# A planned one-core decoder trunk: first loads on two DMA queues in smaller weight pieces, the last row tile in two column halves

## The chip, the cores and the metric

The kernel runs on one core of one Trainium2 chip. The metric is the device time of one execution in microseconds (us); shorter is better. The other seven cores are idle.

## The reference

One layer of a hybrid decoder trunk works on 1,024 prompt tokens and 64 sample tokens (8 sequences of 8), each of width 1,024. Everything is float32.

```
h    = rms_norm(x, norm_g)
proj = h @ w_in                                   # 1024 x 3088: a, gl, zc, q, k, v, zg, lr
u    = a * sigmoid(gl)                            # causal depthwise convolution of width 31 over u,
cv   = silu(group_layer_norm(conv(u)))            # then group LayerNorm, silu and a 512 x 512 product
cv   = (cv @ w_pw + b_pw) * silu(zc)
o    = gated_linear_attention(q, k, v, gates(lr)) # 4 heads, chunked, exact recurrence
o    = rms_norm_per_head(o) * gla_g * silu(zg)
y    = rms_norm(x + concat[cv, o] @ w_out, final_g)
```

Outputs are y, the last 30 rows of u for the prompt and for each sample sequence, and the final attention states.

## The kernel before, in words

Tokens lie in three chunks of columns: `CHUNKS = [(0, 384), (384, 384), (768, 320)]`. The third, `FIRST = 2`, is worked on first. Every matrix is split in two float32r parts (h_ and l_ for weights, hh and hl for activations). ScalarE (ACT) copies the high part, VectorE (DVE) subtracts to get the low part, and TensorE (PE) makes three products for each block of 128 rows: hh by h, hl by h, hh by l.

**Order.** The instructions are not written in their final order. `prog.add` collects them with a priority (the place in the program), and `schedule` (L188) plans an order for each engine from cost estimates: `LAT`, `IN` and `SAME` are latencies in ns, SP is the queue of DMA issues, `STICK` lets TensorE go on with the same type of matmul rather than switch, and `DVE_PACE` lengthens VectorE's estimates. The order planned is what each engine then runs, strictly in turn. Operations that need an activation table are chained in program order (`self.chain`), so that a table is loaded no more often than the program's text demands.

**The start (L1004 to L1026).** Ten matmuls on zeros warm TensorE (tile `warm`). All loads go out on SP. For each half h of the depth and each of four weight tiles (gl and a of column tiles 0 and 1), the loop loads one block of x for `FIRST` (`x_load`, 160 KB), one weight half (`whalf`, four blocks of 128 rows, 256 KB, tile s_gl or s_a) and splits both (`raw_split`: hh on ACT and hl on DVE, from x times norm_g, without the norm; `load_split`: h_ on ACT, l_ on DVE). Four staging tiles `wst` hold weight halves; the last two halves go into `big` tiles. `rms_scale(c)` squares x on ACT (tile sq), adds squares on DVE, sums over partitions with float32 matmuls (tile ms), and makes rs[c] with Ln and Exp on ACT. The products of `FIRST` are scaled by rs afterwards: `gl_chunk` and `a_chunk` with early=True multiply by rs, take the sigmoid and multiply again. Chunks 0 and 1 are normalised first (`rms_split`: x times norm_g times rs on DVE, then a split) and need rs of their chunk. Loads of chunk 1 are held until a matmul of rs[FIRST] has run.

**The end (L1211 to L1350).** The output product is made from seven products of half matrices (pr1 to pr7), 48 matmuls of 512 columns each; the last is pr4, added by `product` into the PSUM banks acc[0..3] (tile ya), one bank for each of the row tiles 4 to 7. `y_first` handles one column half of a row tile: square with a row sum on ACT, multiply by fg (final_g) on DVE, a small operation on ss. `y_last` handles the other half: square with row sum, Ln and Exp for the row's scale, one `scalar_tensor_tensor` on DVE for its own half y, an ACT copy with the scale for the finished half z, and two stores to out_y, both on SP. The last loop goes over the row tiles 4, 5, 6, 7; the last half of tile 6 is stored after tile 7's sum is made (argument `after`).

Of the kernel before, what the change touches and what calls it, by code (L numbers as in the profile page):

```python
# [6 lines left out]
F32 = mybir.dt.float32  # L7
# [128 lines left out]
class Program:  # L136
# [51 lines left out]
    def schedule(self):  # L188
        import heapq
        from bisect import bisect_left, insort  # L190
        LAT = {"PE": 197 + MARGIN, "DVE": 130 + MARGIN, "ACT": 143 + MARGIN, "POOL": 150, "SP": 900}
        IN = {"PE": 129, "DVE": 0, "ACT": 0, "POOL": 0, "SP": 50}
        SAME = {"PE": 0, "DVE": 127, "ACT": 150, "POOL": 60, "SP": 900}
        free_at = {t: [0.0] * n for t, n in self.slots.items()}
        pend = {t: [] for t in self.slots}
        for o in self.ops:
# [14 lines left out]
        table = [next(o.table for o in self.ops if o.table is not None)]  # L211
        tile_end = {}
        holder = {}
        dma = [0.0, 0.0]
        done = []
        kind = [None]

# [12 lines left out]
            return True  # L230

        def cross(d, o):
            if d.eng == o.eng:
                return SAME[o.eng]

            return LAT[d.eng] + IN[o.eng] + (SLACK if o.eng == "PE" and d.eng != "SP" and d.end > SLACK_FROM else 0)

        while events:
            t, e = heapq.heappop(events)
            if t < t_free[e]:  # L240
                continue
            best = same = None
            nxt = None
            for o in avail[e]:
                if o.ready <= t:
                    if (best is None or o.prio < best.prio) and can_alloc(o, t):
                        best = o
                    if (e == "PE" and o.kind == kind[0] and (same is None or o.prio < same.prio)
                            and can_alloc(o, t, True)):
                        same = o  # L250
                elif nxt is None or o.ready < nxt:
                    nxt = o.ready
            if best is None:
                if nxt is not None:
                    heapq.heappush(events, (nxt, e))
                continue

            if same is not None and same.prio < best.prio + STICK:
                best = same
            o = best  # L260
            avail[e].remove(o)
            o.start = t
            cost = o.cost
            if o.table is not None and table[0] != o.table:
                table[0] = o.table
                cost += 1300
            if e == "PE" and o.kind != kind[0]:
                kind[0] = o.kind
                cost += 90
            if e == "SP":  # L270
                t_free[e] = t + 60
                dma[0] = max(dma[0], t) + 450
                dma[1] = max(dma[1], dma[0] + 650) + o.bytes / 360.0
                o.end = dma[1]
            else:
                if e == "DVE":
                    cost *= DVE_PACE
                o.end = t + cost + o.lag
                t_free[e] = t + cost
            done.append(o)  # L280
            for tl in o.tiles:
                if tl.tag in free_at and tl.slot is None:
                    o.allocs.append(tl)
                    k = min(range(len(free_at[tl.tag])), key=lambda i: free_at[tl.tag][i])
                    free_at[tl.tag][k] = float("inf")
                    tl.slot = k
                    tl.before = holder.get((tl.tag, k))
                    holder[(tl.tag, k)] = tl
                    del pend[tl.tag][bisect_left(pend[tl.tag], tl.first)]
                    for e2 in LAT:  # L290
                        heapq.heappush(events, (max(t, t_free[e2]), e2))
            for tl in o.tiles:
                tl.left -= 1
                tile_end[tl] = max(tile_end.get(tl, 0.0), o.end + LAT[e])
                if tl.left == 0 and tl.tag in free_at:
                    free_at[tl.tag][tl.slot] = tile_end[tl]
                    for e2 in LAT:
                        heapq.heappush(events, (max(tile_end[tl], t_free[e2]), e2))
            for u in o.users:
                u.ready = max(u.ready, o.end + cross(o, u))  # L300
                u.wait -= 1
                if u.wait == 0:
                    avail[u.eng].append(u)
                    heapq.heappush(events, (max(u.ready, t_free[u.eng]), u.eng))
            heapq.heappush(events, (t_free[e], e))
# [25 lines left out]
def build(tc, A, O):  # L331
# [9 lines left out]
    def R(v):  # L341
        return v.ap() if isinstance(v, View) else v
# [47 lines left out]
    def zero(out):  # L390
        fill(out, 0.0)

    def dma(out, in_, late=False):
        v = out if isinstance(out, View) else in_
        if late:
            prog.hold = late
        prog.add("SP", lambda: nc.sync.dma_start(R(out), R(in_)), [out], [in_], 0,  # L397
                 nbytes=v.n * 4 * (v.part[1] - v.part[0]))

    def dma_add(out, in_):  # L400
# [19 lines left out]
    with ctx:  # L420
# [37 lines left out]
        def pc(i, n=1):  # L458
            return par[:, i:i + n]
# [20 lines left out]
        hl = [[None] * 3 for _ in range(KT)]  # L480
        xs = {}

        def x_load(c, ks=range(KT), late=False):
            t0, n = CHUNKS[c]
            for k in ks:
                xk = rows("x", k, F32)[:, t0:t0 + n]
                dma(xk, A["xT"][:, k, t0:t0 + n], late)
                xs[(c, k)] = xk

        row_tiles = {}  # L490
# [36 lines left out]
            act(rs[c], ms, AF.Ln, bias=eps)  # L527
            act(rs[c], rs[c], AF.Exp, scale=-0.5)

        def rms_split(c):  # L530
            n = CHUNKS[c][1]
            for k in range(KT):
                xk = xs[(c, k)]
                stt(xk, xk, pc(C_NG + k), rs[c], ALU.mult, ALU.mult)
                hh[k][c], hl[k][c] = part("hh", k, c), part("hl", k, c)
                split(hh[k][c], hl[k][c], xk)
# [10 lines left out]

        def whalf(kind, i, h, stage=None):
            return load_split(f"{kind}{i}_{h}", A["w_in"][mt[(kind, i)]][:, 4 * h:4 * h + 4, :], 4, P, stage)

        def wtile(kind, i):
            return [whalf(kind, i, h) for h in range(2)]
# [448 lines left out]
                mix_samples(4 + i, o[:, 256:n])  # L1001


        dma(par, A["par"])  # L1004
        w0, w1 = [[], []], [[], []]
        for h in range(2):
            for i, (w, kind, ct) in enumerate(((w0[0], "gl", 0), (w0[1], "a", 0), (w1[0], "gl", 1), (w1[1], "a", 1))):
                x_load(FIRST, range(4 * h + i, 4 * h + i + 1))
                w.append(whalf(kind, ct, h, stage=big if 4 * h + i >= STAGE else None))
                raw_split(range(4 * h + i, 4 * h + i + 1))  # L1010
        rms_scale(FIRST)
        x_load(0)
        x_load(1, late=True)
        rms_scale(0)
        for ct, w in enumerate((w0, w1)):
            gl_chunk(ct, w[0], FIRST, True)
            a_chunk(ct, w[1], FIRST, True)
        rms_split(0)
        rms_scale(1)
        rms_split(1)  # L1020
        w_rank = gate_load()
        for c in (0, 1):
            for ct, w in enumerate((w0, w1)):
                gl_chunk(ct, w[0], c)
                a_chunk(ct, w[1], c)
        rms_split(FIRST)  # L1026
        for ct in range(CT):
            dma(u_s[ct][:, :, 0:CW - 1], A["cc"][:, ct], late=True)
        dma(cst, A["cst"], late=True)
# [169 lines left out]
                bv.append(parts(f"{name}b", i, b(i)))  # L1199
            return av, bv  # L1200

        def product(acc, ops, first):
            av, bv = ops
            for t in range(4):
                ts_ = slice(P * t, P * t + P)
                for k in range(4):
                    mm(acc[t], av[k][:, 0, ts_], bv[k][:, 0, :], first and k == 0, False)
                    mm(acc[t], av[k][:, 0, ts_], bv[k][:, 1, :], False, False)
                    mm(acc[t], av[k][:, 1, ts_], bv[k][:, 0, :], False, k == 3)

        pr1 = prep("p1", lambda i: A11[i], lambda i: B11("p", i))  # L1211

# [12 lines left out]
        def y_first(tk, h):  # L1225

            y = xr[(tk, h)]
            rows_ = y.part[1] - y.part[0]
            s_ = ss[tk] = VT(sm, "ss", [P, 4], F32, f"ss{tk}")[:rows_]
            junk = VT(unit, "unit", [P, 512], BF16, f"sq{tk}_{h}")  # L1230
            act(junk[:rows_], y, AF.Square, accum=s_[:, 0:1])
            tt(y, y, fg[:rows_, 512 * h:512 * h + 512], ALU.mult)
            ts(s_[:, 1:2], s_[:, 0:1], 1.0 / DM, eps[:rows_], ALU.mult, ALU.add)

        def y_last(tk, h, after=None):

            y, z, s_ = xr[(tk, h)], xr[(tk, 1 - h)], ss[tk]
            rows_ = y.part[1] - y.part[0]
            junk = VT(unit, "unit", [P, 512], BF16, f"sq{tk}_{h}")
            act(junk[:rows_], y, AF.Square, accum=s_[:, 2:3])  # L1240
            act(s_[:, 3:4], s_[:, 2:3], AF.Ln, scale=1.0 / DM, bias=s_[:, 1:2])
            act(s_[:, 3:4], s_[:, 3:4], AF.Exp, scale=-0.5)
            o = stt(y, y, s_[:, 3:4], fg[:rows_, 512 * h:512 * h + 512], ALU.mult, ALU.mult)
            if after is not None:
                o.deps.add(after)
            act(z, z, AF.Copy, scale=s_[:, 3:4])
            for g_, t_ in ((1 - h, z), (h, y)):
                dma(O["y"][tk * P:tk * P + rows_, 512 * g_:512 * g_ + 512], t_)

        def samples_half(h, first, last, bops, e0, ps=None):  # L1250
            for k in range(4):
# [86 lines left out]
        for t in range(4):  # L1338
# [1 line left out]
            tt(y, p5s[t // 2][:, t % 2, :], y, ALU.add)  # L1340
            tt(y, acc[t], y, ALU.add)
            y_first(4 + t, 1)
        product(acc, pr4, False)
        for t in range(4):
            y = x_tile(4 + t, 0, mark)
            o = tt(y, acc[t], y, ALU.add)
            if t == 3:
                y_last(6, 0, o)
            if t != 2:
                y_last(4 + t, 0)  # L1350

        with tc.manual_schedule():
            dep = mybir.DependencyInfo(mybir.DependencyClass.Sync, mybir.DependencyReason.ANTI)
# [87 lines left out]
```

## Time and profile before

| | us |
|---|---|
| median of 3 runs | 468.67 (468.04 to 469.09) |
| profiled execution, whole | 470.14 |
| span of the profiled execution | 468.4 |
| granted TensorE clock, mean | 0.992 |

The span runs from the first to the last recorded event of the execution; the whole time is 1.74 us longer. TensorE is busy for 457.8 us of the span, VectorE 393.4, ScalarE 307.6. PE is TensorE's matmul, PEld its weight load, SPq the queue of SyncE that issues DMAs. A row of a timeline gives start, duration, engine, line, operation, output and inputs, shape, a count, and in brackets the idle time before it and what ended it.

### The profile page before, as it was taken

What the parts mean: (1) busy time and instruction counts of PE and PEld (TensorE: products, weight loads), DVE (VectorE), ACT (ScalarE), POOL (GpSimd) and SP (SyncE); (2) the same over time, 40 slices, a digit from 0 to 9 for tenths busy, and PEclk for the clock granted to TensorE, in tenths of its full rate; (3) what the DMA queues carried; (4) which work ended last, traced back from release to release, by engine and by line L of the source; (5) the groups of instructions that cost most, each with busy time, mean ns of one, the idle gap of its engine ahead of it and who ended that gap; (6) DMA issues with size and microseconds to landing.
All of it is one profiled execution on the core that took longest, in us unless ns stands there. A gap on an engine that the chain in (4) does not pass through costs nothing.

```text
span 468.4 us, 7544 instructions
## 1 busy us (share of the span) xinstructions
PE 457.8 (98%) x2714; PEld 420.8 (90%) x2714; DVE 393.4 (84%) x627; ACT 307.6 (66%) x769; POOL 19.8 (4%) x38
## 2 busy tenths in 40 slices
PE   7999999999999999999999999999999999999993
PEld 6899989999888899898999999999999988888782
DVE  4899997999999999998999999943538948998863
ACT  6897639974633624567766677653898648879735
POOL 1000000000000000000000000000000023130000
PEclk9999999999999999999999999999999999999998
DMA  8740273141300050002211121011235393385834
GB/s 250 265 146 7 88 167 50 45 59 56 58 0 1 8 171 1 2 22 92 69 57 45 41 97 45 24 59 65 81 78 182 88 226 58 77 180 138 288 127 179
DMA packets 35477, 43.26 MB, mean 92 GB/s; under 512 B 12912, under 2 KB 19824, under 8 KB 35440
## 3 DMA queue, kind: packets, MB, share of 16 engines
q1 hardware_dynamic: 33136, 38.59, 27.2%
q0 software_dynamic: 2304, 4.20, 5.5%
q8 instruction: 21, 0.34, 0.3%
q14 instruction: 16, 0.13, 0.1%
HBM read 36.58 MB, written 6.19 MB: 91 GB/s over the span
## 4 chain that ended last, share of the span: by engine, by line
PE 89%; ACT 3%; DMA 3%; DVE 2%; SPq 1%; issue 1%; DVEq 0%
PE p_zc L409 10%; PE pv L409 10%; PE p_zg L409 10%; PE p_gl L409 10%; PE p_a L409 9%; PE ya L409 7%; PE p_q L409 5%; PE p_k L409 5%; PE pw L409 5%; PE yc L409 5%; PE po L409 2%; PE pys L409 2%; SPq L397 1%; DMA s_gl<-in_w_in 1%; PE pa L409 1%; DMA xr<-in_x 1%
## 5 line engine op out<-in xcount | busy, mean ns | idle before, releaser
L359 DVE SCALAR_TENSOR_TENSOR cv<-u,par,cv 128x1024 f32<-128x1024 f32 x120 | 151.0, 1277 | 0.2
L409 PE MATMUL p_gl<-hh,h_gl 128*128 128x384 f32 (+1 forms) x96 | 32.5, 338 | 1.9 <-ACT h_gl L353 1.0
L353 ACT ACTIVATE pr<-us,par 128x64 f32<-128x64 f32 x124 | 31.9, 341 | 1.2 <-DMA us<-in_cc 1.2
L409 PE MATMUL p_gl<-hl,h_gl 128*128 128x384 f32 (+1 forms) x96 | 31.9, 332 | 0.1
L409 PE MATMUL p_gl<-hh,l_gl 128*128 128x384 f32 (+1 forms) x96 | 32.0, 333 | 0.0
L409 PE MATMUL p_a<-hh,h_a 128*128 128x384 f32 (+1 forms) x96 | 31.9, 332 | 0.0
L409 PE MATMUL p_a<-hl,h_a 128*128 128x384 f32 (+1 forms) x96 | 31.9, 332 | 0.0
L409 PE MATMUL p_a<-hh,l_a 128*128 128x384 f32 (+1 forms) x96 | 31.6, 331 | 0.0
L409 PE MATMUL p_zc<-hl,h_zc 128*128 128x384 f32 (+1 forms) x96 | 31.6, 329 | 0.0
L409 PE MATMUL p_zc<-hh,h_zc 128*128 128x384 f32 (+1 forms) x96 | 31.5, 328 | 0.0
L409 PE MATMUL p_zc<-hh,l_zc 128*128 128x384 f32 (+1 forms) x96 | 31.4, 328 | 0.0
L409 PE MATMUL p_zg<-hh,h_zg 128*128 128x384 f32 (+1 forms) x96 | 31.3, 326 | 0.0
L409 PE MATMUL p_zg<-hl,h_zg 128*128 128x384 f32 (+1 forms) x96 | 31.3, 326 | 0.0
L409 PE MATMUL p_zg<-hh,l_zg 128*128 128x384 f32 (+1 forms) x96 | 31.3, 326 | 0.0
L409 PE MATMUL pv<-h_v,hl 128*128 128x512 f32 x64 | 24.9, 390 | 0.0
L409 PE MATMUL pv<-l_v,hh 128*128 128x512 f32 x64 | 24.9, 389 | 0.0
L409 PE MATMUL pv<-h_v,hh 128*128 128x512 f32 x64 | 24.9, 389 | 0.0
L409 PEld LDWEIGHTS p_gl<-hh,h_gl 128*128 128x128 f32 x96 | 18.4, 191 | 3.0 <-ACT h_gl L353 1.5
L353 ACT ACTIVATE v<-pv 128x512 f32<-128x512 f32 x8 | 4.8, 599 | 21.9 <-PE pv L409 20.1
L409 PEld LDWEIGHTS p_gl<-hl,h_gl 128*128 128x128 f32 x96 | 18.5, 192 | 0.7 <-DVE hl L363 0.4
L409 PEld LDWEIGHTS p_gl<-hh,l_gl 128*128 128x128 f32 x96 | 18.3, 190 | 0.8 <-DVE cv L359 0.4
L363 DVE TENSOR_TENSOR o<-o,zg 128x384 f32<-128x384 f32 (+1 forms) x12 | 6.3, 533 | 14.7 <-ACT zg L353 14.7
(335 smaller groups left out, 1305.2 us busy)
## 6 DMA issues: line engine op xcount, KB each, us to landing
xr<-in_x SPq DMA_DIRECT2D x16, 256.0 KB, 4.1
out_y<-xr SPq DMA_DIRECT2D x16, 256.0 KB, 2.3
x<-in_xT SPq DMA_DIRECT2D x16, 192.0 KB, 4.1
T<-in_w_out POOLq DMA_DIRECT2D x12, 256.0 KB, 5.2
s_gl<-in_w_in SPq DMA_DIRECT2D x8, 256.0 KB, 5.1
s_a<-in_w_in SPq DMA_DIRECT2D x8, 256.0 KB, 3.9
s_v<-in_wv SPq DMA_DIRECT2D x16, 128.0 KB, 2.2
s_zc<-in_w_in SPq DMA_DIRECT2D x8, 256.0 KB, 3.0
```

The costliest lines, as they stand in the source:

```text
L353: return S.activation(R(out), R(in_), func, **kw)
L359: return prog.add("DVE", lambda: V.scalar_tensor_tensor(R(out), R(a), R(s), R(b), op0, op1), [out], [a, s, b], out.n / 0.96 + 67 + 62 * is ...
L363: return prog.add("DVE", lambda: V.tensor_tensor(R(out), R(a), R(b), op), [out], [a, b], out.n / 0.96 + 67)
L397: prog.add("SP", lambda: nc.sync.dma_start(R(out), R(in_)), [out], [in_], 0, nbytes=v.n * 4 * (v.part[1] - v.part[0]))
L409: o = prog.add("PE", lambda: T.matmul(R(ps), R(lhsT), R(rhs), start=start, stop=stop, skip_group_check=True), [ps], [lhsT, rhs], c / share ...
```

## The change

The first loads go out on two queues: par and the first weight pieces on ACT's queue, the rest on SP's. The weight halves of the first half of the depth are loaded and split in two pieces of two row blocks each (128 KB), those of the second half whole. `rms_split(0)` and `rms_scale(1)` move ahead of the products of `FIRST` in the program, so in priority; with that, Ln and Exp of chunk 1 come ahead of the first sigmoids in the chain of tables. `rms_split(FIRST)` is held until chunk 0's first product has been issued. At the end, row tile 7's last product is made in two column halves of 256, the first in a fresh bank (acd[3]); the earlier content of its columns in acc[3] is added to the row tile beforehand. `y_part` squares the first half early. Row tile 6's finished half z is scaled by VectorE (`ts`) rather than ACT, after tile 7's sum. Row tile 7's two stores go out on ACT's and SP's queue. In the planner, SP's latency falls from 900 to 700, DMA times are estimated by another formula, ACT's DMA issues are known, and `STICK` and `DVE_PACE` hold only from 45 us of the plan on.

```diff
-        LAT = {..., "SP": 900}
+        LAT = {..., "SP": 700}
-            if same is not None and same.prio < best.prio + STICK:
+            if same is not None and t > SLACK_FROM and same.prio < best.prio + STICK:
...
-            if e == "SP":
-                t_free[e] = t + 60
-                dma[0] = max(dma[0], t) + 450
-                dma[1] = max(dma[1], dma[0] + 650) + o.bytes / 360.0
-                o.end = dma[1]
+            if o.bytes and e != "POOL":
+                t_free[e] = t + 450
+                dma_end = max(dma_end, t + 1000) + o.bytes / (250.0 if t < 4500 else 350.0)
+                o.end = dma_end
             else:
-                if e == "DVE":
+                if e == "DVE" and t > SLACK_FROM:
                     cost *= DVE_PACE
...
-        dma(par, A["par"])
+        dma(par, A["par"], eng="ACT")
         w0, w1 = [[], []], [[], []]
         for h in range(2):
-            for i, (w, kind, ct) in enumerate(((w0[0], "gl", 0), (w0[1], "a", 0), (w1[0], "gl", 1), (w1[1], "a", 1))):
-                x_load(FIRST, range(4 * h + i, 4 * h + i + 1))
-                w.append(whalf(kind, ct, h, stage=big if 4 * h + i >= STAGE else None))
-                raw_split(range(4 * h + i, 4 * h + i + 1))
+            parts_ = []
+            for w, kind, ct in ((w0[0], "gl", 0), (w0[1], "a", 0), (w1[0], "gl", 1), (w1[1], "a", 1)):
+                tiles, piece = whalf_parts(kind, ct, h, big if 4 * h + len(parts_) >= STAGE else None)
+                w.append(tiles)
+                parts_.append(piece)
+
+            n = 2 if h == 0 else 4
+            for j in range(0, 4, n):
+                for i, piece in enumerate(parts_):
+                    if i < n:
+                        k = 4 * h + j + i
+                        x_load(FIRST, range(k, k + 1))
+                        raw_split(range(k, k + 1))
+                    piece(j, j + n, "ACT" if h + j == 0 else "SP")
         rms_scale(FIRST)
         x_load(0)
         x_load(1, late=True)
         rms_scale(0)
+        rms_split(0)
+        rms_scale(1)
         for ct, w in enumerate((w0, w1)):
             gl_chunk(ct, w[0], FIRST, True)
             a_chunk(ct, w[1], FIRST, True)
-        rms_split(0)
-        rms_scale(1)
         rms_split(1)
...
                 gl_chunk(ct, w[0], c)
+                begun = begun or prog.last_pe
                 a_chunk(ct, w[1], c)
-        rms_split(FIRST)
+        rms_split(FIRST, begun)
...
+            def piece(a, b, eng):
+                dma(st[:, a:b, :], src[:, 4 * h + a:4 * h + b, :], eng=eng)
+                split(hi[:, a:b, :], lo[:, a:b, :], st[:, a:b, :])
...
+        def y_part(tk, y):
+
+            s_ = ss[tk]
+            y_square(tk, y, 4)
+            stt(s_[:, 1:2], s_[:, 4:5], 1.0 / DM, s_[:, 1:2], ALU.mult, ALU.add)
...
             if after is not None:
                 o.deps.add(after)
-            act(z, z, AF.Copy, scale=s_[:, 3:4])
-            for g_, t_ in ((1 - h, z), (h, y)):
-                dma(O["y"][tk * P:tk * P + rows_, 512 * g_:512 * g_ + 512], t_)
+                ts(z, z, s_[:, 3:4], None, ALU.mult, None)
+            else:
+                act(z, z, AF.Copy, scale=s_[:, 3:4])
+            for g_, t_, q_ in ((1 - h, z, eng), (h, y, "SP")):
+                dma(O["y"][tk * P:tk * P + rows_, 512 * g_:512 * g_ + 512], t_, eng=q_)
...
-        product(acc, pr4, False)
-        for t in range(4):
-            y = x_tile(4 + t, 0, mark)
-            o = tt(y, acc[t], y, ALU.add)
-            if t == 3:
-                y_last(6, 0, o)
-            if t != 2:
-                y_last(4 + t, 0)
+
+        ends = [slice(0, 256), slice(256, 512)]
+        ys = [x_tile(4 + t, 0, mark) for t in range(4)]
+        tt(ys[3][:, ends[0]], acc[3][:, ends[0]], ys[3][:, ends[0]], ALU.add)
+        product(acc, pr4, False, range(3))
+        product(acd, pr4, True, [3], ends[0])
+        product(acc, pr4, False, [3], ends[1])
+        for t in range(3):
+            tt(ys[t], acc[t], ys[t], ALU.add)
+            if t < 2:
                 y_last(4 + t, 0)
+        tt(ys[3][:, ends[0]], acd[3][:, ends[0]], ys[3][:, ends[0]], ALU.add)
+        y_part(7, ys[3][:, ends[0]])
+        o = tt(ys[3][:, ends[1]], acc[3][:, ends[1]], ys[3][:, ends[1]], ALU.add)
+        y_last(6, 0, o)
+        y_last(7, 0, None, ends[1], "ACT")
```

## Rows read from the trace of the kernel before

**Rows 1.** The page's first part: busy time, share of the span and instructions.
```profile
PE 457.8 (98%) x2714; PEld 420.8 (90%) x2714; DVE 393.4 (84%) x627; ACT 307.6 (66%) x769; POOL 19.8 (4%) x38
```

**Rows 2.** Stretches: length, busy time (count) by engine, granted clock, DMA, GB/s.
```profile
5.00:10.00 5.00, 3.11 (x13) 2.00 (x12) 2.73 (x6) 3.18 (x7) 0.00 (x0) 0.99 0.95 312
10.00:15.00 5.00, 5.00 (x24) 5.00 (x25) 4.70 (x9) 5.00 (x12) 0.00 (x0) 0.67 0.96 331
...
461.00:469.00 8.00, 0.00 (x0) 0.00 (x0) 2.16 (x3) 3.23 (x10) 0.00 (x0) 0.68 0.48 180
```

**Rows 3.** Waits of PE, 0 to 70 us: total, times, longest.
```profile
PE p_gl L409 <- ACT h_gl L353: 1.0, 1, 1.0
```

**Rows 4.** Timeline of the first 14 us: warm-up, first loads, first products.
```profile
0.75 1.28 ACT L315 ACT_TABLE_LOAD   x1 [0.75 <-PEq L1432]
0.75 0.39 SPq L397 DMA_DIRECT2D par<-in_par  x1
...
1.07 4.34 PEld L409 LDWEIGHTS warm<-warm 128*128 128x128 f32 x20 [1.07 <-DVE warm L469]
...
1.19 0.42 SPq L397 DMA_DIRECT2D x<-in_xT  x1
...
3.75 0.56 ACT L353 ACTIVATE hh<-x,par 128x320 fp32r<-128x320 f32 x1 [1.72 <-DMA x<-in_xT]
...
5.66 0.64 PE L409 MATMUL p_gl<-hh,h_gl 128*128 128x320 f32 x1
...
10.00 0.63 PE L409 MATMUL p_gl<-hh,h_gl 128*128 128x320 f32 x1 [1.03 <-ACT h_gl L353]
...
13.10 0.40 PE L409 MATMUL p_gl<-hl,h_gl 128*128 128x320 f32 x1
```

**Rows 5.** DMA of the first 30 us, 40 slices: busy tenths, GB/s.
```profile
DMA  0049899987999999999999999721186998999930
GB/s 0 0 105 216 236 303 290 253 243 219 342 387 401 367 345 343 361 292 309 324 361 284 330 348 388 287 101 33 25 303 171 365 240 223 311 341 330 356 143 11
```

**Rows 6.** Timeline, 22 to 41 us: rs, chunk 0's first product, chunk 1's rs.
```profile
22.01 0.53 ACT L353 ACTIVATE rs<-ms,par 128x320 f32<-128x320 f32 x1 [1.73 <-PE ms L409]
...
27.44 0.34 PE L409 MATMUL p_gl<-hh,h_gl 128*128 128x384 f32 x1
...
40.90 0.51 ACT L353 ACTIVATE rs<-rs 128x384 f32<-128x384 f32 x1
```

**Rows 7.** The chain that ended last, in order: start, length, what.
```profile
14.08 1.91 PE p_gl L409 x13
...
54.27 4.16 PE p_gl L409 x24
...
413.70 10.88 PE ya L409 x48
...
443.75 4.50 DMA xr<-in_x
```

**Rows 8.** Timeline of the last 19 us: last product, row tiles 4 to 7.
```profile
449.89 11.04 PE L409 MATMUL ya<-p4b,p4a 128*128 128x512 f32 x48
...
454.33 0.68 DVE L363 TENSOR_TENSOR xr<-ya,xr 128x512 f32<-128x512 f32 x1
...
459.74 0.68 DVE L363 TENSOR_TENSOR xr<-ya,xr 128x512 f32<-128x512 f32 x1
...
460.97 0.69 DVE L363 TENSOR_TENSOR xr<-ya,xr 128x512 f32<-128x512 f32 x1 [0.55 <-PE ya L409]
...
461.21 0.53 ACT L353 ACTIVATE ss<-ss 128x1 f32<-128x1 f32 x2
...
461.77 0.72 ACT L353 ACTIVATE xr<-xr,ss 128x512 f32<-128x512 f32 x1
...
463.70 0.75 DVE L359 SCALAR_TENSOR_TENSOR xr<-xr,ss,fg 128x512 f32<-128x512 f32 x1 [1.18 <-ACT ss L353]
...
464.45 0.81 SPq L397 DMA_DIRECT2D out_y<-xr  x2
```

More of the change, by code (lines that the diff above doesn't have):

```diff
@@ L190, in schedule @@
         from bisect import bisect_left, insort
-        LAT = {"PE": 197 + MARGIN, "DVE": 130 + MARGIN, "ACT": 143 + MARGIN, "POOL": 150, "SP": 900}
+        LAT = {"PE": 197 + MARGIN, "DVE": 130 + MARGIN, "ACT": 143 + MARGIN, "POOL": 150, "SP": 700}
         IN = {"PE": 129, "DVE": 0, "ACT": 0, "POOL": 0, "SP": 50}
-        SAME = {"PE": 0, "DVE": 127, "ACT": 150, "POOL": 60, "SP": 900}
+        SAME = {"PE": 0, "DVE": 127, "ACT": 150, "POOL": 60, "SP": 700}
         free_at = {t: [0.0] * n for t, n in self.slots.items()}
@@ L213, in schedule @@
         holder = {}
-        dma = [0.0, 0.0]
+        dma_end = 0.0
         done = []
@@ L232, in cross @@
         def cross(d, o):
+            if d.eng == "ACT" and d.bytes:
+                return LAT["SP"] + IN[o.eng]
             if d.eng == o.eng:
@@ L391, in zero, with dma @@
         fill(out, 0.0)
-    def dma(out, in_, late=False):
+    def dma(out, in_, late=False, eng="SP"):
         v = out if isinstance(out, View) else in_
@@ L396, in dma @@
             prog.hold = late
-        prog.add("SP", lambda: nc.sync.dma_start(R(out), R(in_)), [out], [in_], 0,
+        q = nc.sync if eng == "SP" else S
+        prog.add(eng, lambda: q.dma_start(R(out), R(in_)), [out], [in_], 0,
                  nbytes=v.n * 4 * (v.part[1] - v.part[0]))
@@ L481, in build, with x_load @@
         xs = {}
-        def x_load(c, ks=range(KT), late=False):
+        def x_load(c, ks=range(KT), late=False, eng="SP"):
             t0, n = CHUNKS[c]
@@ L486, in x_load @@
                 xk = rows("x", k, F32)[:, t0:t0 + n]
-                dma(xk, A["xT"][:, k, t0:t0 + n], late)
+                dma(xk, A["xT"][:, k, t0:t0 + n], late, eng)
                 xs[(c, k)] = xk
@@ L528, in rms_scale, with rms_split @@
             act(rs[c], rs[c], AF.Exp, scale=-0.5)
-        def rms_split(c):
+        def rms_split(c, wait=None):
             n = CHUNKS[c][1]
@@ L533, in rms_split @@
                 xk = xs[(c, k)]
+                if wait is not None:
+                    prog.hold = wait
                 stt(xk, xk, pc(C_NG + k), rs[c], ALU.mult, ALU.mult)
@@ L549, in whalf, with whalf_parts @@
             return load_split(f"{kind}{i}_{h}", A["w_in"][mt[(kind, i)]][:, 4 * h:4 * h + 4, :], 4, P, stage)
+        def whalf_parts(kind, i, h, stage=None):
+            name, src = f"{kind}{i}_{h}", A["w_in"][mt[(kind, i)]]
+            st = VT(stage or wst, "big" if stage else "wst", [P, 4, P], F32, f"s_{name}")
+            hi = VT(wh, "wh", [P, 4, P], F32R, f"h_{name}")
+            lo = VT(wl, "wl", [P, 4, P], F32R, f"l_{name}")
+            def piece(a, b, eng):
+                dma(st[:, a:b, :], src[:, 4 * h + a:4 * h + b, :], eng=eng)
+                split(hi[:, a:b, :], lo[:, a:b, :], st[:, a:b, :])
+            return (hi, lo), piece
         def wtile(kind, i):
@@ L1017, in build @@
             a_chunk(ct, w[1], FIRST, True)
-        rms_split(0)
-        rms_scale(1)
         rms_split(1)
         w_rank = gate_load()
+        begun = None
         for c in (0, 1):
@@ L1200, in prep, with product @@
             return av, bv
-        def product(acc, ops, first):
+        def product(acc, ops, first, tiles=range(4), c=slice(0, 512)):
             av, bv = ops
-            for t in range(4):
+            for t in tiles:
                 ts_ = slice(P * t, P * t + P)
                 for k in range(4):
-                    mm(acc[t], av[k][:, 0, ts_], bv[k][:, 0, :], first and k == 0, False)
-                    mm(acc[t], av[k][:, 0, ts_], bv[k][:, 1, :], False, False)
-                    mm(acc[t], av[k][:, 1, ts_], bv[k][:, 0, :], False, k == 3)
+                    mm(acc[t][:, c], av[k][:, 0, ts_], bv[k][:, 0, c], first and k == 0, False)
+                    mm(acc[t][:, c], av[k][:, 0, ts_], bv[k][:, 1, c], False, False)
+                    mm(acc[t][:, c], av[k][:, 1, ts_], bv[k][:, 0, c], False, k == 3)
         pr1 = prep("p1", lambda i: A11[i], lambda i: B11("p", i))
@@ L1228, in y_first @@
             rows_ = y.part[1] - y.part[0]
-            s_ = ss[tk] = VT(sm, "ss", [P, 4], F32, f"ss{tk}")[:rows_]
+            s_ = ss[tk] = VT(sm, "ss", [P, 5], F32, f"ss{tk}")[:rows_]
             junk = VT(unit, "unit", [P, 512], BF16, f"sq{tk}_{h}")
@@ L1233, in y_first, with y_square, y_last @@
             ts(s_[:, 1:2], s_[:, 0:1], 1.0 / DM, eps[:rows_], ALU.mult, ALU.add)
-        def y_last(tk, h, after=None):
+        def y_square(tk, y, i):
+            junk = VT(unit, "unit", [P, 512], BF16, f"sq{tk}_{i}")[:y.part[1] - y.part[0], :y.n]
+            act(junk, y, AF.Square, accum=ss[tk][:, i:i + 1])
+        def y_part(tk, y):
+            s_ = ss[tk]
+            y_square(tk, y, 4)
+            stt(s_[:, 1:2], s_[:, 4:5], 1.0 / DM, s_[:, 1:2], ALU.mult, ALU.add)
+        def y_last(tk, h, after=None, part=None, eng="SP"):
             y, z, s_ = xr[(tk, h)], xr[(tk, 1 - h)], ss[tk]
             rows_ = y.part[1] - y.part[0]
-            junk = VT(unit, "unit", [P, 512], BF16, f"sq{tk}_{h}")
-            act(junk[:rows_], y, AF.Square, accum=s_[:, 2:3])
+            y_square(tk, y if part is None else y[:, part], 2)
             act(s_[:, 3:4], s_[:, 2:3], AF.Ln, scale=1.0 / DM, bias=s_[:, 1:2])
@@ L1342, in build @@
             y_first(4 + t, 1)
-        product(acc, pr4, False)
-        for t in range(4):
-            y = x_tile(4 + t, 0, mark)
-            o = tt(y, acc[t], y, ALU.add)
-            if t == 3:
-                y_last(6, 0, o)
-            if t != 2:
-                y_last(4 + t, 0)
+        ends = [slice(0, 256), slice(256, 512)]
[7 more added lines that the diff above has]
+            if t < 2:
+                y_last(4 + t, 0)
+        tt(ys[3][:, ends[0]], acd[3][:, ends[0]], ys[3][:, ends[0]], ALU.add)
[3 more added lines that the diff above has]
+        y_last(7, 0, None, ends[1], "ACT")
         with tc.manual_schedule():
```

## The prediction

> **What bounds the kernel now.** I read the page's busy shares first: TensorE is busy for 98% of the span, so only the few microseconds in which it isn't, or runs slowly, and the tail behind its last matmul can be won [rows 1]. Then the stretches show where they lie: little runs between 5 and 10 us, the granted clock is 0.67 between 10 and 15, and TensorE has nothing to do behind 461 [rows 2]. The view of its waits up to 70 us names the longest: an ACT split of a gl weight half, which waited for its load [rows 3]. From 30 to 460 us that view is empty. So what the start gives reaches the end, unless the new plan opens a gap in between.
>
> **The start, as it is.** The first product of FIRST issues at 5.66, the next unbroken run begins at 10.00 [rows 4]. I count nine products between them. One takes 1.91 / 13 = 0.147 us at the full clock [rows 7], so 4.34 us did 1.3 us of work: 3.0 lost. Then eleven starts fill 10.00 to 13.10 [rows 4], where the work is 1.6: another 1.5 us lost at the lower of the two clock levels, right after the gaps. The warm-up ends at 1.07 + 4.34 = 5.41 [rows 4], before which nothing can start: 0.25 more. In all 4.7 us for TensorE.
>
> **What the new loads do.** Today the first k blocks need four weight halves of 256 KB and two x blocks of 160 KB: 1.37 MB. With pieces it is four times 128 KB and the x blocks, 0.85 MB, for 24 products. The DMA view's slices (0.75 us each) add up to about 1.4 MB by 7.5 us and 0.86 MB by 5.25 [rows 5], so the data of those 24 products can be there some 2 us sooner. SP's further pieces share the same engines, so I expect them between 5 and 7 rather than all at 5.25. After that one block of x with its four weight blocks is 0.43 MB for twelve products: 1.76 us of TensorE against 1.4 to 1.7 us at 250 to 300 GB/s. Supply and use about balance, the gaps close, and with no gaps I expect the clock to stay up.
>
> The Trainium skill (DMA: Bandwidth & Descriptors, Issuing engines are not separate DMA queues) says that a second issuing engine saves only issue time, as all DMAs interleave on the same engines. The trace agrees: the engines were 80 to 90% busy from 3 us on at 216 to 303 GB/s [rows 5], with SP's issues only 0.4 us long [rows 4]. By that rule alone the start gains 0.44 us, the time by which x's first issue moves up.
>
> My sum takes no bandwidth from the second queue. What counts is which bytes come first.
>
> **What TensorE waits for next: ACT.** Chunk 0 starts at 27.44 [rows 6]. Were TensorE alone the limit it would start at 27.44 - 4.7 = 22.7. But chunk 0's split needs rs of chunk 0, and ACT has all of FIRST's splits and two chunks of squares ahead of it. ACT was busy for all of 10 to 15 us; it was idle for 5.00 - 3.18 = 1.82 us in 5 to 10 [rows 2], and for 1.73 before rs at 22.01 [rows 6]. Only these 3.55 us can be closed. Against that the change splits four halves into eight ACT copies. The trace has no 256-column copy; its fixed part lies between nothing and half of a 320-column one (0.56, [rows 4]), 0 to 0.28 each. I take 0.1, so 0.4 in all, nearer the lower end because rows of these engines mostly scale with length. The five issues on ACT fall where it waited anyway, 2.03 to 3.75 [rows 4], at some 0.43 each: about nothing if they run beside the table load, up to 0.5 if they start behind it. Start: 3.55 - 0.4 = **3.1 us gained**; bounds 0.4 (only the issue slot) and 4.7.
>
> **Order of the splits, planner, tables.** Raising `rms_split(0)`, holding `rms_split(FIRST)` and two table loads fewer (1.28 each, [rows 4]) take work off ACT and VectorE behind 23 us. TensorE waits for next to nothing there, so I give them nothing; they are cover for the 3.1, without which chunk 0's splits would come too late. Chunk 1 needs its rs, which ended at 41.41 [rows 6]. Chunk 0 is four groups of 4.16 us [rows 7], so TensorE wants chunk 1 at 24.3 + 16.6 = 40.9, which rs must now beat by a split, and I think it does: it no longer stands behind a sigmoid table and FIRST's split. Behind 45 us the plan's rules change only in DMA times. VectorE is 84% busy over the whole span [rows 1], so a replan may open or close small gaps: 0, with 0.5 either way.
>
> **The end.** TensorE ends at 449.89 + 11.04 = 460.93, the last pair of stores issues from 464.45 [rows 8]. Twelve matmuls of 512 columns (10.88 / 48 = 0.227 each) become 24 of 256. Columns of 320, 384 and 512 cost 0.147, 0.173, 0.227 [rows 7], which continues to 0.120: 2.88 against 2.72, 0.16 us more; at the nearest measured form, 0.147, it is 0.8 more. Tile 7's chain took 463.70 - 460.97 = 2.73 from sum to final scaling, 0.72 of it behind tile 6's ACT copy [rows 8], which moves to VectorE. Halving the sum and the square saves about 0.5. If TensorE set the end, the stores would issue 0.72 + 0.5 - 0.16 = 1.0 us sooner.
>
> I don't think it does. Row tile 4's products end at 449.89 + 2.72 = 452.61, its sum runs at 454.33; tile 6's could run at 458.05 and runs at 459.74: VectorE is 1.7 us late [rows 8], and the ending chain goes back through a load of xr that took 4.50 us [rows 7]. The edits don't hasten that load. VectorE runs in order: tile 6's sum (459.74), tile 7's first half (to about 460.8), then the small operation of `y_part`, which waits for ACT's square of that half, and behind it the second half. ACT has tile 6's square until 461.21, then Ln and Exp of 0.53 [rows 8]. The new square follows at 461.2 or 461.75, some 0.55 long; the small operation ends at 462.0 or 462.5; the second half's sum at 462.4 or 462.95; its square, Ln and Exp at 463.5 or 464.05; scaling 0.75 more, 464.25 or 464.8. Against 464.45 that is -0.2 to +0.35. The two stores issuing at once save little, as the first's data already cover the second's issue. The extra sum of half a tile (under 0.69) ahead of all this may add 0.4. I take **0** for the end, bounds -1.0 and +0.8.
>
> **Sum.** Against the profiled execution's 470.14: 470.14 - 3.1 = 467.0. It stands 1.47 above the median, so the median comes to 468.67 - 3.1 = **465.6**.
>
> **Rivals.**
> *A, as above*, 464.6 to 466.8: 0.53.
> *B, the end gains as well*: xr arrives early enough, TensorE sets the end, 1.0 more: 464.6, down to 463.6. For it: tile 7's sum did wait for TensorE by 0.55 [rows 8]. Against it: tile 6's lateness. 0.21.
> *C, the bytes come no sooner*: par and the pieces issue behind the table load (it ends at 2.03, [rows 4]), or pieces and SP's loads share the engines so that the four weights come together again. Only the 0.44 remains, 468.2; with half of the gaps closed, 467.3. For it: the engines were already near busy [rows 5]. 0.17. The Trainium skill's rule above would end here.
> *D, slower, by the chain of tables*: FIRST's sigmoids now stand behind rs of chunk 1. If that rs stays at 41.41, TensorE runs out of chunk 0 at 40.9, waits about 0.6 for the split behind it and holds banks of unfinished products. It is slower than before once rs comes later than about 44: 3.1 us of waiting eat the gain, and as behind the first gaps, 1.5 more go to the lower clock: 468.67 + 1.5 = 470.2. For it: rs stands behind eight splits of VectorE. Against: a table load less. 0.09.
>
> The range takes A, B and the nearer half of C, 0.82 in all: 463.6 to 467.9. About 0.2% (0.94 us) is what a measurement can tell from no change. Faster: A, B and a third of C, 0.79; same: the rest of C, 0.12; slower: 0.09.
>
> **What would show it.** Right: a first product at 5.4, no wait of TensorE above 0.5 us before 20, a granted clock near 1.0 in 10 to 15, and chunk 0's first product at about 24.3. Wrong: ACT's first issue behind 2.03, a gap at 7 to 10, or TensorE waiting at about 41. At the end: tile 7's second sum behind the small operation by the wait on ACT confirms the 0; its sum right behind TensorE's last matmul means B.

## The result, and the profile after

The change made the kernel slower: 473.81 us median (472.76 to 474.25) against 468.67 (467.80 to 469.61) in the same comparison, a ratio of 1.0104 [1.0085, 1.0123]. The forecast was 465.6, 463.6 to 467.9. The profiled execution of the changed kernel is its fastest one (472.76, span 470.6), that of before was a long one (470.14), so the two traces show 2.2 us of span where the medians are 5.1 apart.

The page's busy shares, as in [rows 1]; then the stretches of [rows 2] with the same columns:

```profile
PE 456.6 (97%) x2726; PEld 420.2 (89%) x2726; DVE 393.4 (84%) x635; ACT 305.0 (65%) x772; POOL 20.0 (4%) x38
```

```profile
5.00:10.00 5.00, 3.40 (x14) 2.86 (x13) 3.84 (x10) 4.58 (x13) 0.00 (x0) 0.78 0.88 282
10.00:15.00 5.00, 5.00 (x32) 5.00 (x32) 5.00 (x13) 5.00 (x13) 0.00 (x0) 0.88 0.88 286
...
461.00:469.00 8.00, 0.00 (x0) 0.00 (x0) 4.00 (x8) 4.15 (x13) 0.00 (x0) 0.76 0.57 214
```

TensorE does 1.2 us less, and more of the start's products lie before 15 us (46 against 37). Its granted clock was 0.78 and 0.88 in the first two stretches, 0.99 and 0.67 before; the forecast was near 1.0 in the second. Behind 461 us VectorE works 4.00 us where it was 2.16, ACT 4.15 where it was 3.23: the tail has grown.

The start: timeline of the first 9 us (answers to [rows 4]), and the DMA slices up to 30 us ([rows 5]).

```profile
0.75 1.28 ACT L316 ACT_TABLE_LOAD   x1 [0.75 <-PEq L1480]
0.75 1.34 SPq L399 DMA_DIRECT2D x<-in_xT  x3
0.78 0.40 ACTq L399 DMA_DIRECT2D par<-in_par  x1
...
1.21 0.45 ACTq L399 DMA_DIRECT2D s_gl<-in_w_in  x1
...
1.69 0.45 ACTq L399 DMA_DIRECT2D s_a<-in_w_in  x1
...
4.55 0.33 ACTq L399 DMA_DIRECT2D s_gl<-in_w_in  x1
4.92 0.44 ACTq L399 DMA_DIRECT2D s_a<-in_w_in  x1
5.42 0.56 ACT L354 ACTIVATE hh<-x,par 128x320 fp32r<-128x320 f32 x1 [3.38 <-DMA x<-in_xT]
...
6.69 0.41 PE L411 MATMUL p_gl<-hh,h_gl 128*128 128x320 f32 x1 [1.57 <-ACT h_gl L354]
```

```profile
DMA  0049979986899778989999999999999998212220
GB/s 0 0 65 318 294 238 331 364 307 202 209 318 285 186 204 299 326 312 353 300 380 397 404 398 386 365 379 396 356 367 389 361 355 309 105 30 32 27 23 6
```

ACT's first three issues run beside the table load. Its fourth comes 2.4 us behind the third, at 4.55, and the first split of x stands behind the fifth. The wait in its bracket is put down to x, but ACT had left its own queue only at 5.36. The first product came at 6.69, where it was 5.66 before and 5.4 in the forecast; the 1.57 us in front of it are TensorE's longest wait behind the warm-up (1.0 before, [rows 3]). The bytes came a little sooner than in [rows 5]: the slices of 0.75 us add up to 0.93 MB by 5.25 us and 1.59 MB by 7.5, against 0.86 and 1.40.

Chunk 0 and rs of chunk 1 ([rows 6]): the first product of chunk 0 came 0.9 us earlier than before, not 3.1, and rs of chunk 1 ended at 38.42 rather than 41.41. The first row is rs of chunk 0, 0.5 us later than before (second fence); the product is earlier all the same, because TensorE had done FIRST's products sooner and waited only 0.22 us for chunk 0's split.

```profile
23.44 0.58 ACT L354 ACTIVATE rs<-ms,par 128x384 f32<-128x384 f32 x1 [1.18 <-PE ms L411]
...
26.55 0.45 PE L411 MATMUL p_gl<-hh,h_gl 128*128 128x384 f32 x1 [0.22 <-ACT hh L354]
...
37.91 0.51 ACT L354 ACTIVATE rs<-rs 128x384 f32<-128x384 f32 x1
```

```profile
22.95 0.56 ACT L353 ACTIVATE rs<-ms,par 128x384 f32<-128x384 f32 x1
```

The end: the chain that ended last ([rows 7]) and the timeline ([rows 8]).

```profile
405.64 1.04 ACT T L354 x2
407.14 5.28 DMA s_b12u<-in_w_out
418.54 1.28 DVE p7a L364 x2
421.65 4.70 DMA s_b12p<-in_w_out
432.23 1.28 ACT L320
437.77 3.66 DMA xr<-in_x
...
444.97 5.58 DMA xr<-in_x
```

```profile
458.49 1.60 PE L411 MATMUL ya<-p4b,p4a 128*128 128x256 f32 x12
...
464.09 0.16 DVE L360 SCALAR_TENSOR_TENSOR ss<-ss 128x1 f32<-128x1 f32 x1 [1.18 <-ACT sq L354]
...
464.58 0.42 DVE L364 TENSOR_TENSOR xr<-ya,xr 128x256 f32<-128x256 f32 x1
...
466.89 0.39 ACTq L399 DMA_DIRECT2D out_y<-xr  x1
```

In [rows 7] the chain runs on TensorE until SP issues a load of xr (443.75). Here it leaves TensorE some 40 us earlier, for two loads of w_out (s_b12u, s_b12p), then ACT and its table load, and then the loads of xr. TensorE ended at 460.09, 0.8 earlier than before, and the last stores issued 6.8 behind that (before 464.45 - 460.93 = 3.5). The two largest groups of ACT's waits for loads between 375 and 440 us say which: the first fence is the kernel before, the second the one after. Then ACT's timeline, before and after. s_b12u and s_b12p are staging tiles of w_out; p3, p4 and p7 are inputs of the third, fourth and seventh half product.

```profile
ACT p7b L353 <- DMA s_b12u<-in_w_out: 1.4, 3, 0.6
ACT s_b12u L353 <- DMA s_b12u<-in_w_out: 0.8, 2, 0.6
```

```profile
ACT s_b12u L354 <- DMA s_b12u<-in_w_out: 3.6, 4, 2.5
ACT b L354 <- DMA s_b12p<-in_w_out: 2.4, 1, 2.4
```

```profile
411.57 0.62 ACT L353 ACTIVATE p3a<-S 128x512 fp32r<-128x512 f32 x1
...
415.70 0.63 ACT L353 ACTIVATE s_b12u<-s_b12u 128x512 f32<-128x512 f32 x1
...
417.77 0.63 ACT L353 ACTIVATE s_b12u<-s_b12u 128x512 f32<-128x512 f32 x1 [0.62 <-DMA s_b12u<-in_w_out]
```

```profile
409.39 0.60 ACT L354 ACTIVATE p5s<-yc 128x512 f32<-128x512 f32 x1 [2.18 <-PE yc L411]
412.53 0.63 ACT L354 ACTIVATE s_b12u<-s_b12u 128x512 f32<-128x512 f32 x1 [2.54 <-DMA s_b12u<-in_w_out]
413.07 0.61 ACT L354 ACTIVATE p3a<-S 128x512 fp32r<-128x512 f32 x1
...
426.37 0.63 ACT L354 ACTIVATE b<-s_b12p 128x512 fp32r<-128x512 f32 x1 [2.44 <-DMA s_b12p<-in_w_out]
```

ACT stood at a load while the splits of p3, whose data was there, queued behind it. In the kernel before these splits ran first (from 411.57), and ACT then met the load nearly landed. The second wait is a place of the same kind: the first split of b stands ahead of two splits of p7b, where before all of p7b came first. No edit touches this code: the planner's new numbers put it in another order.

### The profile page after: what moved, and what is told of

Read it like the earlier page. It is cut to its first block, busy times and chain, and to the rows that moved or that the text cites. A ratio compares the mean times of both kernels' runs of the same rounds, so it can differ in the third digit from the quotient of the medians.

```text
span 470.6 us, 7587 instructions
## 1 busy us (share of the span) xinstructions
PE 456.6 (97%) x2726; PEld 420.2 (89%) x2726; DVE 393.4 (84%) x635; ACT 305.0 (65%) x772; POOL 20.0 (4%) x38
## 4 chain that ended last, share of the span: by engine, by line
PE 77%; DMA 8%; ACT 7%; DVE 4%; issue 2%; SPq 1%; DVEq 0%; ACTq 0%
PE p_zc L411 10%; PE p_zg L411 10%; PE pv L411 9%; PE p_gl L411 9%; PE p_a L411 8%; PE p_q L411 5%; PE p_k L411 5%; PE pw L411 5%; PE ya L411 4%; DMA x<-in_xT 3%; PE po L411 2%; DMA xr<-in_x 2%; DVE xr L364 2%; ACT sq L354 2%; DMA s_b12u<-in_w_out 1%
## 5 line engine op out<-in xcount | busy, mean ns | idle before, releaser
L411 PEld LDWEIGHTS p_a<-hh,l_a 128*128 128x128 f32 x96 | 18.3, 191 | 0.4
L354 ACT ACTIVATE sq<-xr 128x512 bf16<-128x512 f32 (+2 forms) x19 | 11.4, 600 | 11.1 <-DVE xr L364 11.1
```

The lines of the kernel that those rows point to most:

```text
L354: return S.activation(R(out), R(in_), func, **kw)
L411: o = prog.add("PE", lambda: T.matmul(R(ps), R(lhsT), R(rhs), start=start, stop=stop, skip_group_check=True), [ps], [lhsT, rhs], c / share ...
```

## The experiments

All were timed in five rounds beside the kernel before (468.7 to 469.5 in the four groups); each ratio is to that, and goes by all executions, not by the two medians. Theory P: the late part of the new plan, made with lower DMA times, places ACT's work ahead of its loads, and that costs the end. Theory L: ACT's own DMA issues hold it up at the start. The rivals are the edits of the start (theory S) and of the end (theory E) by themselves.

### One part at a time

**The planner alone** (kernel before with SP at 700, the new formula, and STICK and DVE_PACE from 45 us on).

> The kernel before with the planner's new numbers alone (SP latency 700, new DMA formula, STICK and DVE_PACE from 45 us of the plan on); loads, splits and the end are as before. Theory P (the plan): the new numbers make loads look earlier than they land, ACT and VectorE are queued behind late loads between 400 and 435 us, the stores and the xr loads behind them slip: 471.5 to 474, with ACT waits on s_b12u or s_b12p above 2 us. Theory E (the edited end costs by itself): 468 to 469.5. Theory S (the new start costs): 468 to 469.5.

475.29, ratio 1.0161 [1.0117, 1.0205]: a loss at least as large as the change's, with no edit to any instruction, and above theory P's 474. The profiled execution is one of its two long ones (479.55). In it ACT waits 4.1 for s_b12u and 2.8 for s_b12p; in addition TensorE stood 3.9 us for one split of v.

```profile
PE pv L408 <- DVE l_v L362: 3.9, 1, 3.9
```

**The change with the old DMA numbers** (`"SP": 900` and the old formula, for the whole plan).

> The changed kernel with SP's latency and the DMA formula in the planner put back (ACT's issues by the same old formula). Theory P: most of the loss goes, 466 to 469. Theory E: stays at 472 to 474.5, the end still runs late. Theory S: stays at 472 to 474.5.

474.86, 1.0118 [1.0094, 1.0142]: theory P's 466 to 469 missed. The end was good (last stores 2.6 us behind TensorE), but the first product came only at 10.43. The old numbers order the new start badly.

**The start alone** (new loads and order, `STICK` and `DVE_PACE` from 45 us on, old DMA numbers).

> The kernel before with the new start alone (two queues, pieces, moved splits, STICK and DVE_PACE gated), old DMA numbers in the planner, old end. Theory P: 466.5 to 468.5, the start gives up to 1 us, as ACT still waits in its own DMA issues. Theory E: 466.5 to 468.5. Theory S: 471 to 474.

473.92, 1.0099 [1.0078, 1.0120]: inside theory S's 471 to 474, above theory P's. What costs is the start as the old numbers order it; ordered by the new ones, below, it costs nothing. It is the same start as in the run before, and this part of the timeline shows it: ACT is off its queue at 5.1, makes three splits of x before the first of gl, and TensorE waits 4.7.

```profile
4.67 0.45 ACTq L400 DMA_DIRECT2D s_a<-in_w_in  x1
5.16 0.56 ACT L355 ACTIVATE hh<-x,par 128x320 fp32r<-128x320 f32 x1 [3.13 <-DMA x<-in_xT]
...
5.99 1.00 ACT L355 ACTIVATE hh<-x,par 128x320 fp32r<-128x320 f32 x2
6.89 0.40 ACT L355 ACTIVATE h_gl<-s_gl 128x256 fp32r<-128x256 f32 x1
...
10.38 0.64 PE L412 MATMUL p_gl<-hh,h_gl 128*128 128x320 f32 x1 [4.68 <-ACT h_gl L355]
```

**The end alone** (column halves, `y_part`, VectorE's scaling, two store queues).

> The kernel before with the new end alone (tile 7 in two halves, stores on two queues, tile 6 scaled by VectorE), old start and old planner numbers. Theory P: 467.5 to 469.5, near nothing. Theory E: 470.5 to 473. Theory S: 467.5 to 469.5.

469.86, 1.0004 [0.9986, 1.0022]: nothing. Tile 7's second half stands behind the small operation, as the prediction's chain has it, and the store issues at 464.42 (forecast 464.25 to 464.8):

```profile
461.62 0.16 DVE L361 SCALAR_TENSOR_TENSOR ss<-ss 128x1 f32<-128x1 f32 x1 [1.18 <-ACT sq L355]
...
464.42 0.40 ACTq L400 DMA_DIRECT2D out_y<-xr  x1
```

### Only the late part of the plan

**The change, old numbers behind 45 us.** New numbers still order the start:

```diff
+                if t > SLACK_FROM:
+                    t_free[e] = t + (60 if e == "SP" else 450)
+                    dma = max(dma, t) + 450
+                    dma_end = max(dma_end, dma + 650) + o.bytes / 360.0
```

and `cross` adds 200 to SP's latency there (`LATE_SP = 900`).

> The changed kernel, but the planner reckons with the new DMA numbers only up to 45 us of the plan; later loads get the old latency of 900 and the old formula. Theory P (the new numbers place ACT and VectorE work ahead of the loads that it needs behind 45 us, which costs the 3 us at the end): ACT's waits for s_b12u and b, 6.0 us in the changed kernel, fall to about 1; the first store behind TensorE's last matmul comes 3 to 4 us after it rather than 6.8; start as in the changed kernel (first product near 6.7, about 0.6 us ahead at 65 us); time 468 to 470. Rival R (the end is late for another reason: the start on two queues or any new order): the tail stays at 6 us or more and the time at 472 to 475.

469.1, 0.9992 [0.9973, 1.0012]. P holds: s_b12u is waited for only by p7b (1.4), TensorE's last product ends at 458.58, the last store issues 3.7 later. The new start, in the new numbers' order, is in this version, so theory S is out for the start as the change has it.

**The kernel before, new numbers behind 45 us.**

> The kernel before, with the new DMA latency and formula only behind 45 us of the plan; the order of the start is untouched. Theory P: ACT waits for s_b12u and b again for 4 us or more, the stores come 6 to 7 us behind TensorE's last matmul, time 471 to 474. Rival (the slower plan-only run lost its time in the first 45 us, by STICK and VectorE's pace): time 468.5 to 470 and ACT's waits as in the kernel before.

472.52, 1.0077 [1.0048, 1.0107]: a like loss in a kernel that is otherwise the old one. ACT waits 3.7 for s_b12u and 2.6 for s_b12p. What the planner alone lost beyond this (1.0161) comes from its rules for the first 45 us (DMA numbers, `STICK`, `DVE_PACE`); which of them it is, beyond the 3.9 us for v in one long execution, stays open.

**The kernel before, SP's late latency at 1800.**

> The kernel before, with SP's latency in the plan raised from 900 to 1800 behind 45 us: a dose in the other direction. Theory P: what is planned behind a load comes later still, ACT's waits for s_b12u and b (2.2 us in the kernel before) fall under 1, the time is that of before or up to 1 us less (467.5 to 469.5). Rival (any new order of the late part costs time, whatever its numbers): 471 or more.

467.93, 0.9975 [0.9959, 0.9990]: a little faster than before, so a replan by itself isn't what costs. The mechanism expected here didn't show: ACT's waits for s_b12u were 2.7 us in all, not under 1 (2.2 before), so where this gain comes from stays open.

**One of the two numbers at a time**: first only the latency set back to 900 behind 45 us, then only the formula.

> The changed kernel with SP's latency back at 900 behind 45 us, the new DMA formula kept. If the cause is the 0.2 us of latency, ACT's waits for s_b12u and b fall to about 1.5 and the time to 469 to 470, as when both were set back (469.1). If it is the formula (450 ns for each issue on SP, a start 0.1 us earlier), the time stays at 472 to 474. If both count by their 0.2 and 0.1 us, 470 to 471.5.

> The changed kernel with the old DMA formula behind 45 us and the new latency of 700 kept: the other half of the pair. By the latency alone 472 to 474 with ACT's waits at 5 us or more; by the formula alone 469 to 470; by both 470.5 to 472.

469.44, 0.9989 [0.9966, 1.0012], and 469.65, 1.0007 [0.9985, 1.0028]. Setting back either is enough: neither new number costs anything by itself, the two together do, and in both traces the splits of p3 again run ahead of s_b12u. A part of the loss from each, the third case of both expectations, is out; this spoke for a decision that flips when a load is thought some 0.3 us earlier (0.2 by the latency, 0.1 by the formula) but not yet at 0.2, rather than for a sum of delays.

### The one decision

**The change with one dependency more.** All numbers of the planner stay new.

```diff
+        n3 = len(prog.ops)
         pr3 = prep("p3", s4, lambda i: B22("p", i))
+        a3 = [o for o in prog.ops[n3:] if o.eng == "ACT"]
...
+        n7 = len(prog.ops)
         pr7 = prep("p7", s3, t3)
+        a7 = [o for o in prog.ops[n7:] if o.eng == "ACT"]
+        a7[1].deps.add(a3[-1])
```

> The changed kernel with one dependency more: ACT's first scaling of s_b12u comes after the last split of p3; all the planner's numbers stay new. Theory Q (one flipped decision carries the loss: ACT stands 2.5 us at that load, and what is behind it on ACT, stores, xr loads and the last row tiles, comes later): ACT's waits for s_b12u and b fall from 6.0 us to about 1.5, the stores come 2.5 to 4 us after TensorE's last matmul, time 468.5 to 470. Rival (the loss is the sum of many places of the new order): 471 to 474.

468.07, 1.0006 [0.9979, 1.0032], a little under the 468.5 to 470 expected: the whole loss is gone (the change had 1.0104). The two s_b12u scalings that come first no longer wait, ACT's table load is at 427.73 (432.23 in the change), and the last store issues 2.4 us behind TensorE (459.48). ACT's wait for s_b12u, and the rows of the timeline:

```profile
ACT s_b12u L354 <- DMA s_b12u<-in_w_out: 1.1, 2, 0.8
```

```profile
409.98 0.62 ACT L354 ACTIVATE p3a<-S 128x512 fp32r<-128x512 f32 x1
...
414.10 1.19 ACT L354 ACTIVATE s_b12u<-s_b12u 128x512 f32<-128x512 f32 x2
...
427.73 1.28 ACT L320 ACT_TABLE_LOAD   x1
...
457.88 1.60 PE L411 MATMUL ya<-p4b,p4a 128*128 128x256 f32 x12
...
461.88 0.38 ACTq L399 DMA_DIRECT2D out_y<-xr  x1
```

The pin moves other places too, since the planner goes on from it: the b splits then came behind all of p7b, as in the kernel before. So it tests the two places together, the one pinned and the one that follows from it in the plan.

**The kernel before, with the bad place pinned** (`for o in a3[2:]: o.deps.add(a7[1])`).

> The kernel before with all its numbers, but the second to fourth pair of the p3 splits on ACT only after the first scaling of s_b12u, as the changed kernel has it. Theory Q: ACT waits about 2.5 us for s_b12u, the tail behind TensorE's last matmul grows from 3.5 us to 5 to 7, time 471 to 473. Rival: 468.5 to 470, the wait is made up before the end.

471.78, 1.0073 [1.0054, 1.0092]: the old numbers with this order make a like loss. The first split of b came ahead of splits of p7b again. The waits of the change are back, and the chain ends at 465.02 + 0.75, 5.4 us behind TensorE's last product (460.40).

```profile
ACT s_b12u L353 <- DMA s_b12u<-in_w_out: 4.5, 4, 2.4
...
ACT b L353 <- DMA s_b12p<-in_w_out: 1.8, 1, 1.8
```

### ACT's own issues

**Old late numbers, and only par and the first two pieces on ACT** (`"ACT" if h + j == 0 and i < 2 else "SP"`).

> As the run before, and only par and the first pieces of gl and a of column tile 0 are issued on ACT; the first pieces of column tile 1 go out on SP. Theory L (ACT's fourth and fifth issue stand until an earlier transfer has ended, and hh behind them): ACT is free at about 2.1 rather than 5.3, hh of the first block of x starts when that block lands, 3.4 to 4.1, first product 5.4 rather than 6.7, time 1 to 1.5 us less than the run before. Rival (the bytes come no sooner): first product near 6.5 still, behind the load of s_gl, and the same time within 0.4 us.

468.28, 0.9979 [0.9957, 1.0001], 0.8 less than with four pieces (1 to 1.5 expected), a difference that the intervals don't separate. The mechanism is seen in the trace: ACT is free behind its third issue, and split and product come 1.5 us earlier.

```profile
1.68 0.45 ACTq L406 DMA_DIRECT2D s_a<-in_w_in  x1
...
3.85 0.56 ACT L361 ACTIVATE hh<-x,par 128x320 fp32r<-128x320 f32 x1 [1.82 <-DMA par<-in_par]
...
5.13 0.42 PE L418 MATMUL p_gl<-hh,h_gl 128*128 128x320 f32 x1
```

**The same with everything on SP.**

> Old numbers behind 45 us; the first loads in the new order and in pieces, but all of them and par on SP. What the second queue itself gives: if only the order and size of the pieces count, within 0.5 us of the version with two pieces on ACT (468.3), first product at 5.1 to 5.6. If issue time counts (par and two pieces cost SP three issues of about 0.45 us before x), first product 1 us later, at 6 to 6.5, and 0.5 to 1 us more, 469 to 469.3.

468.91, 0.9998 [0.9974, 1.0021], first product at 5.36. In these profiles ACT's queue brings the first product forward by 0.2 us at most (5.13). The profiled execution was a long one (471.35), with 2.5 us in which TensorE stood for a split of v, so the 0.6 us between the two medians can't be put down to the queue. The Trainium skill (DMA: Bandwidth & Descriptors, Issuing engines are not separate DMA queues) says that a second issuing engine saves issue time alone; this run agrees.

**Two pieces on ACT, with the late latency at 1800, and with the pin.**

> The start with two pieces on ACT, and SP's latency 1800 behind 45 us: the two edits that each gained, together. If the gains of start and late order add up (0.8 from two pieces rather than four, 1.2 from 1800 rather than 900 on the kernel before), 466.5 to 467.5. If the late order's gain was already had by setting the numbers back, 468 to 468.5 as with 900.

> The pin of the first run, and only par and two first pieces on ACT. If both causes found are all that the changed kernel loses, the time is that of the version with the old late numbers and two pieces (468.3, or 467.5 to 469), 0.5 to 1.5 us less than the first run.

467.71, 0.9963 [0.9943, 0.9982], and 467.31, 0.9972 [0.9955, 0.9989]: both beat the kernel before, by 0.3 to 0.4%. Whether the gains of start and late order add up isn't settled: the first interval holds the sum of both (0.9954) and 1800 alone (0.9975).

## Why the prediction was wrong

**The step that failed** is the one on order, planner and tables: "Behind 45 us the plan's rules change only in DMA times. ... so a replan may open or close small gaps: 0, with 0.5 either way". In the kernel before, the new numbers behind 45 us alone cost 0.8% (ratio 1.0077), some 3.6 us; in the change, the pin brought 1.0104 back to 1.0006. I bounded it by VectorE's share and by TensorE's empty list of waits, and didn't ask which engine stands in its planned order before a load. ACT, 66% busy in [rows 1], was that engine: 2.5 us of standing at one load, another 2.4 at the next, and then stores, xr loads and row tiles in a line behind it. The numbers taken out of the change and put into the kernel before, the pin and its reverse show it; how the 6.0 us of ACT's waits become 3 to 5 us at the end I only read from the chain (table load 4.5 us later than with the pin, last stores 5.0 later).

**The start** failed in two terms. "The five issues on ACT fall where it waited anyway, ... about nothing if they run beside the table load" took each issue at 0.43. Three did cost that. The fourth and fifth carry a wait, here in the program's list of ACT's instructions:

```
4 L399 DMA s_a_0_101<-in_w_in 128x256
5 L399 DMA s_gl_0_111<-in_w_in 128x256 [waits DMAHW1_49]
6 L399 DMA s_a_0_116<-in_w_in 128x256 [waits DMAHW3_49]
7 L354 ACTIVATE hh_125<-x_88,par 128x320 [waits DMAHW0_49]
```

In this list a DMA reports its end on one of eight counters, DMAHW0 to 7, taken in turn by both queues; the ninth to the twenty-second issue each wait until the counter's last transfer has landed. In the trace the last part of the second x block, which is on DMAHW1, landed at 4.53, and ACT's fourth issue began at 4.55. On SP nothing else stands behind such a wait, on ACT all splits do. The other term is "Only these 3.55 us can be closed". ACT started 5.42 - 3.75 = 1.67 later, worked 15.76 us instead of 15.31 up to rs of chunk 0 (0.45 more, forecast 0.4), and idled 2.26 instead of 3.89: 1.67 + 0.45 - 1.63 = 0.5 us late, 23.44 against 22.95. The wait of rs for the sums on TensorE (1.73 in [rows 6]) didn't close in this execution: it was 2.3 in two pieces, and 1.6 with ACT free early. That its closing follows from an earlier start was argued, not shown. The pinned kernel has the new start and the new end in it and gives 1.0006: together they are worth nothing measurable, not 3.1 us.

**A size from one draw.** The 1.5 us lost to the lower clock in [rows 2] is not in every execution: the kernel with the bad place pinned has the start of before instruction for instruction on TensorE, and had a granted clock of 1.00 in both stretches. The first product of pl, which follows in the plan, starts at 64.96 in the profile of before and at 63.05 in that one (65.04 and 63.79 in the two runs of the kernel before with other late numbers). So up to 1.9 of the 4.7 us that I counted as lost belong to the draw. So does the 1.73 of rs: that wait is none to 1.9 us in five profiles of the old start and 0.5 to 2.3 in five of the new one as the change orders it. The first product of pl starts at 63.05 to 65.18 in those of the old start and at 63.45 to 64.39 in those of the new one, which overlap: no gain of the start shows there. Nor is 5.41, the end of the warm-up, the earliest start: with ACT free early the first product came at 5.13.

**What was right:** the end's 0, with its chain and its times; rs of chunk 1 in time; no issue behind the table load. Rival D forecast a slower kernel, but by an rs of chunk 1 that was not late (38.42), so its direction is luck. The pinned version's interval holds rival C's 468.2 and no gain at all alike. The rival that did come, a late wait of ACT that only the plan's order makes, was not on the list.

## What to carry to other kernels

When a change touches a planner's numbers, compare the planned order of every engine at each load, all the way to the end, and price each place where a strict queue now meets a load before it has landed; two shifts of 0.2 and some 0.1 us in estimates, neither of which cost anything alone, cost some 3.6 us together here, and one dependency took it back. Issue loads from an engine that also computes only as long as no issue has to wait for an earlier transfer; here this moved the first product by 1.5 us, and the time by no more than the intervals hold. Size a loss that hangs on the clock or on the first transfers from several executions, not from one.

## What the runs showed of the hardware

- ACT issued DMAs at 0.78, 1.21 and 1.69 us while its table load ran from 0.75 to 2.03: the load doesn't hold up the queue.
- The 256-column copies that the trace of before lacked take 0.40 us on ACT; twelve matmuls of 256 columns take 1.60 us, and the 24 of tile 7 take 3.03 us (forecast 2.88).
- The same start on the same program order draws its first split of x at 3.75, 3.79, 4.32, 4.48 and 4.71 us in five profiles (the kernel before, and four versions that keep its start), and TensorE is up to 2.1 us apart at 65 us.
